# GpSimd's tensor work moved to VectorE, and a matmul cost in the list scheduler, in a two-block transformer kernel

## The chip, the cores and the metric

The kernel runs on one core of a Trainium2 chip. The metric is the device time of one execution in microseconds (us); lower is better. Measurements of this kernel repeat within about 0.1%.

## The reference

Two transformer blocks follow each other on 512 tokens of width 1024, in float32. Cut to what matters:

```
def first_block(x, c, ctx, ...):
    mod, mod_c = silu(c) @ w_ada + b_ada, silu(c_ctx) @ w_ada + b_ada     # shifts, scales, gates
    hc = modulate(rmsnorm(ctx, norm1_g), csh1, csc1)                       # context keys and values
    h = modulate(rmsnorm(x, norm1_g), sh1, sc1)
    q, k, v, hv, hx1, hx2, gna, ghy = split(h @ w_in)
    y_na = neighbourhood_attention(q, k, v, k_c, v_c, na_rpb)
    y_hy = hyena_mixer(hv, hx1, hx2, ...)          # short conv, sin-MLP filters, two long convs (DFT)
    x = x + g1 * gated_merge(gna, ghy, y_na, y_hy, w_na_o, w_hy_o, w_out)
    x = x + g2 * swiglu(modulate(rmsnorm(x, norm2_g), sh2, sc2), ffn_w1, ffn_w3, ffn_w2)
    return rmsnorm(x, final_g)

def second_block(x, mem, positions, ...):
    c_q, c_kv, k_r, u_ssm, x_q, gate_logits = split_combined(rmsnorm(x) @ w_in)
    y_a = mla_branch(...) @ w_o_mla                # latent attention, causal
    y_b = s5_branch(...) @ w_o_ssm                 # a complex linear recurrence over the tokens
    y_c = cross_branch(x_q, mem, ...) @ w_o_cross
    x = x + (gates0 * y_a + gates1 * y_b + gates2 * y_c) @ w_out
    g_ff, v_ff = split(causal_dwconv(rmsnorm(x) @ w_up))
    return x + (silu(g_ff) * v_ff) @ w_down
```

## The kernel before

**Rounded products.** A float32 matrix product is made of three products of rounded operands (type fp32r). ScalarE copies a tile into a rounded one (the high part), another engine subtracts it from the original (the low part, itself rounded), and TensorE accumulates high x high, high x low and low x high in a PSUM bank (`split`, `lo`, `mm`). Weights come in tiles of 128 x 1024 (`stream`): a load, a ScalarE cast and a subtraction for each tile, and then eight 128 x 128 stationary blocks, each used for 3 products of 128 x 512. Activations pass through the same split after each stage, in tiles of 128 x 512 (`pair`).

**No order is written by hand.** The program first records every instruction as a `Call` on an engine (`Trace.add`), with the pieces of memory that it reads and writes. `Trace.schedule` then plays a list schedule over the calls with a price for each (`Trace.time`) and a lag between engines; `Trace.plan` does this four times, forwards and backwards, and keeps the order with the shortest planned end; `emit` issues the calls in that order. Every instruction therefore has the source line of `emit`, L687, in the profile, and each engine runs its own queue strictly in the emitted order. SBUF is 96 pages of 128 x 512 in 48 segments (the tile `pages`), PSUM eight banks (`banks`), small columns lie in `small`; a call that needs a new page waits in the plan until one is free.

**Which engine.** Most calls name their engine. `may_swap` makes a `tensor_tensor` of VectorE or GpSimd with over 64 elements a row and no operand in PSUM a call of either engine; the plan sends it to GpSimd where it expects it to end there no later than on VectorE. Such calls are the `lo` subtractions, sums of squares, products in `cmul`, gates. Smaller `nc.gpsimd.tensor_tensor` and `tensor_copy` calls are GpSimd's outright. The plan lets a VectorE and a GpSimd instruction run side by side at full price each. A rounded product of n columns costs `n / 2.4 + 2.5` ns on TensorE in the plan, or `cols / 1.2` where that is more.

**Places that the prediction speaks of.** (1) `filters`, at the start: a two-layer sine MLP; each layer ends on VectorE with `sin_arg` (a range reduction of seven instructions of 128 x 256) and a sine on ScalarE; these calls are "urgent", so VectorE takes no others until they are done. Then come the splits of filter weights and DFT matrices, the modulation vectors, the first norm and the context norm (to 147 us). (2) `neighbourhood`, `branch_hy`, `merge1` and the norm of the memory tokens (338 to 530 us). (3) `s5`: products of the state input with phases, two scans over the chunks, and eight products or sums of 128 x 16 x 63 or 64 x 16 x 63 elements before TensorE can go on. (4) `mla`: per token block a small reciprocal square root in eight-element steps (`rsqrt`) and the eviction of heads from PSUM (`heads_to_rows`, 96 x 2 x 128).

```
def lo(self, out, src, hi, pool=None):
    e = self.nc.either if pool is None else self.nc.gpsimd if pool else self.nc.vector
    e.tensor_tensor(out=out, in0=src, in1=hi.bitcast(F32), op=ALU.subtract)
...
V.tensor_tensor(out=fr(F[0]), in0=fr(Z[0]), in1=fr(es if z else ec), op=ALU.mult)
G.tensor_tensor(out=fr(F[1]), in0=fr(Z[1]), in1=fr(ec if z else es), op=ALU.mult)
```

The functions that the diff touches, and what calls them:

Of the kernel before, what the change touches and what calls it, by code (L numbers as in the profile page):

```python
# [161 lines left out]
def layout(inp):  # L162
# [80 lines left out]
ENGINES = ("tensor", "vector", "scalar", "gpsimd", "sync")  # L243
# [7 lines left out]
    (1500.0, 2000.0, 1000.0, 1300.0, 2250.0),  # L251
)
ALONE = (DVE,)
DMA_START = 1700.0
RELEASE = 200.0, 150.0, 150.0, 100.0, 1200.0
TABLES = {AF.Silu: (0,), AF.Sin: (1, 0), AF.Exp: (2,), AF.Gelu_apprx_tanh: (3,)}
TABLE_LOAD = 1283.0
TICK, TICK_COLUMNS = 10240 / 3, 3060.0

# [70 lines left out]
class Call:  # L330
    __slots__ = ("engines", "engine", "name", "args", "kw", "time", "rank", "deps", "then", "waits", "pieces", "begun", "urgent", "start", "number", "tables", "columns")

# [127 lines left out]
class Trace:  # L460
# [15 lines left out]
    def time(engine, name, out, args, kw):  # L476

        n = out.free_size()
        if engine == PE:
            cols = args[1].ap.free_size()  # L480
            if name == "transpose":
                return max(2 * n / 2.4, 53)
            if args[1].ap.dtype == F32R:
                return max(n / 2.4 + 2.5, cols / 1.2)
            return max(4 * n / 2.4 + 2.5, cols / 0.6 if n < 16 else cols / 0.3 if cols > 64 else 54)
# [8 lines left out]
    @staticmethod  # L494
    def may_swap(engines, name, kw):

        views = [kw[n] for n in ("out", "in0", "in1") if n in kw]
        return engines in ((DVE,), (POOL,)) and name == "tensor_tensor" and kw["out"].ap.free_size() > 64 and not any(v.piece.bank for v in views)

    def add(self, engines, name, args, kw):  # L500
        if self.may_swap(engines, name, kw):
            engines = (DVE, POOL)
        c = Call()
# [7 lines left out]
        if name == "tensor_reduce" or name.startswith("reduce") or "accum_out" in kw:  # L511
            big = max((bare(x) for x in (*reads, *writes)), key=lambda x: x.free_size())
        c.time = [self.time(e, name, big, args, kw) for e in engines]
        deps, pieces = set(), {}
        for views, write in ((reads, False), (writes, True)):
# [19 lines left out]
    def schedule(self, order, back=False):  # L535
# [13 lines left out]
        fresh = [True] * len(ENGINES)  # L549
        until = [0.0] * len(ENGINES)  # L550
        events = []
        table = None
# [18 lines left out]
        while left or events:  # L571
            for e in range(len(ENGINES)):
                if not idle[e] or not (fresh[e] or e == POOL):
                    continue
                fresh[e], aside = False, []
                while ready[e]:
# [32 lines left out]
                    if not back:  # L609
# [3 lines left out]
                        if e == PE:  # L613
# [6 lines left out]
                            ticks[i + 1] += (1 - part) * c.columns  # L620
                    idle[e], until[e], fresh[e] = False, now + dur, True
                    n += 1
                    push(events, (now + dur, n, 0, c.number))
                    break
                for key in aside:
                    push(ready[e], key)
            if not events:
                if again:
                    return None
                again, fresh = True, [True] * len(ENGINES)  # L630
                continue
            again = False
            now = events[0][0]
            while events and events[0][0] <= now:
                _, _, kind, i = pop(events)
                c = calls[i]
                if kind == 2:
# [1658 lines left out]
```

## Time and profile before

| | |
|---|---|
| median of 3 runs | 1800.73 us (1799.32 to 1801.01) |
| the profiled execution | 1804.63 us, of which the span from first to last instruction is 1802.8 us |
| TensorE (PE) busy | 1720.8 us, 95% of the span, 8494 products |
| VectorE (DVE) busy | 1219.3 us, 68%, 2245 instructions |
| ScalarE (ACT) busy | 724.4 us, 40% |
| GpSimd (POOL) busy | 363.2 us, 20%, 297 instructions |
| moved by DMA | 235.44 MB, 130 GB/s over the span |
| mean granted TensorE clock | 0.984 of full speed |

TensorE is busy nearly all the time, so what can be won is mostly its 82 us of idle time, the stretches at half clock, and the start. An idle gap of TensorE names what ended it; VectorE ends most of them.

### The profile page before, as it was taken

The numbers are of one execution on the slowest core, as the hardware profiler recorded it, in microseconds if no ns is written. First come the engines' busy times: TensorE is split into PE (matmuls) and PEld (weight loads), VectorE is DVE, ScalarE is ACT, GpSimd is POOL, SyncE is SP. The second block draws the span as 40 slices with busy tenths as digits, with TensorE's granted clock in tenths as the row PEclk, the third lists the DMA queues.
The fourth block names the chain that finished last, engine by engine and source line by source line (L and its number), as shares of the span: only waits on it lengthen the run. The fifth ranks groups of instructions, "written<-read, shape, count | busy, mean of one in ns | idle before, by whom it ended". The sixth has DMA issues, their size and how long they took to land.

```text
span 1802.8 us, 23185 instructions
## 1 busy us (share of the span) xinstructions
PE 1720.8 (95%) x8494; PEld 1423.4 (79%) x8494; DVE 1219.3 (68%) x2245; ACT 724.4 (40%) x1199; POOL 363.2 (20%) x297
## 2 busy tenths in 40 slices
PE   4899999999979999999999999899989999999999
PEld 2478888788868888888888887788867888888887
DVE  7987794888897559435268636649998535896520
ACT  5543333655644222233234431445564413453320
POOL 6631321312240006101011002203242000120000
PEclk9899999999989999999999999999999999999999
DMA  6743233544842623424326434422257222221430
GB/s 224 251 139 117 82 130 108 195 146 141 307 173 104 222 100 94 131 97 137 115 79 208 136 111 126 141 71 72 71 174 270 105 82 71 79 74 70 139 113 18
DMA packets 93664, 235.44 MB, mean 131 GB/s; under 512 B 18316, under 2 KB 26252, under 8 KB 93550
## 3 DMA queue, kind: packets, MB, share of 16 engines
q1 hardware_dynamic: 93550, 233.95, 37.9%
q8 instruction: 67, 1.10, 0.2%
q14 instruction: 47, 0.39, 0.1%
HBM read 206.91 MB, written 27.00 MB: 130 GB/s over the span
## 4 chain that ended last, share of the span: by engine, by line
PE 81%; DVE 10%; DMA 2%; issue 2%; ACT 1%; SPq 0%; POOL 0%; DVEq 0%; POOLq 0%; ACTq 0%
PE banks L687 81%; DVE pages L687 8%; DVE small L687 1%; DMA pages<-in_w_out_dram 1%; ACT pages L687 1%; SPq L687 0%; DMA pages<-in_w_xq_dram 0%; DMA pages<-in_w_mem_dram 0%; DVE banks L687 0%; DMA pages<-s5g 0%; DMA pages<-in_w_ada_dram 0%; POOL pages L687 0%; DMA ud<-pages 0%; DVE gs L687 0%; DVE mod L687 0%
## 5 line engine op out<-in xcount | busy, mean ns | idle before, releaser
L687 PE MATMUL banks<-pages,pages 128*128 128x512 f32 (+6 forms) x7835 | 1676.5, 373 | 58.5 <-DVE pages L687 46.0
L687 PEld LDWEIGHTS banks<-pages,pages 128*128 128x128 f32 (+3 forms) x7835 | 1350.1, 186 | 335.6 <-DVE pages L687 57.5
L687 DVE TENSOR_TENSOR pages<-pages,pages 128x1024 fp32r<-128x1024 f32 (+12 forms) x574 | 572.5, 1020 | 114.2 <-ACT pages L687 102.7
L687 ACT CAST pages<-pages 128x1024 fp32r<-128x1024 f32 (+5 forms) x471 | 398.3, 871 | 399.2 <-DVE pages L687 93.8
L687 POOL TENSOR_TENSOR pages<-pages,pages 128x512 fp32r<-128x512 f32 (+11 forms) x187 | 306.9, 1650 | 939.8 <-ACT pages L687 538.2
L687 DVE TENSOR_TENSOR pages<-banks,pages 128x512 fp32r<-128x512 f32 (+8 forms) x219 | 111.4, 522 | 117.0 <-PE banks L687 91.5
L687 DVE TENSOR_TENSOR pages<-banks,R 128x512 f32<-128x512 f32 x81 | 57.0, 707 | 131.1 <-PE banks L687 130.8
L687 ACT ACTIVATE pages<-pages 128x512 f32<-128x512 f32 (+4 forms) x91 | 50.4, 570 | 168.2 <-DVE pages L687 158.5
L687 ACT ACTIVATE pages<-banks 128x512 f32<-128x512 f32 (+4 forms) x75 | 37.3, 511 | 181.4 <-PE banks L687 154.4
L687 ACT COPY pages<-banks 128x512 f32<-128x512 f32 (+6 forms) x121 | 57.8, 502 | 103.1 <-PE banks L687 100.8
L687 DVE SCALAR_TENSOR_TENSOR pages<-pages,vec,pages 128x511 f32<-128x511 f32 (+3 forms) x120 | 94.0, 801 | 6.9 <-ACT pages L687 5.8
L687 ACT ACTIVATE pages<-pages,vec 128x512 f32<-128x512 f32 (+1 forms) x84 | 63.4, 766 | 68.0 <-DVE pages L687 66.8
L687 DVE TENSOR_TENSOR pages<-pages,banks 128x512 f32<-128x512 f32 x66 | 43.9, 681 | 60.1 <-PE banks L687 58.5
L687 PE MATMUL banks<-ident,pages 128*128 128x128 f32 (+2 forms) x464 | 72.5, 276 | 7.2 <-DVE pages L687 5.7
L687 POOL MEMSET pages<- 128x1 f32 (+4 forms) x63 | 28.9, 482 | 236.8 <-PE banks L687 135.3
L687 PEld LDWEIGHTS banks<-ident,pages 128*128 128x128 f32 (+2 forms) x464 | 56.5, 145 | 22.5 <-issue 5.6
L687 ACT CAST pages<-banks 128x512 fp32r<-128x512 f32 (+5 forms) x118 | 53.2, 469 | 37.5 <-PE banks L687 26.6
L687 ACT ACTIVATE pages<-banks,small 128x512 f32<-128x512 f32 (+3 forms) x80 | 46.4, 585 | 24.9 <-DVE small L687 24.5
L687 DVE SCALAR_TENSOR_TENSOR pages<-pages,pages 128x1024 bf16<-128x1024 f32 (+2 forms) x39 | 52.8, 1367 | 0.1
L687 DVE SCALAR_TENSOR_TENSOR pages<-banks,mod,pages 128x512 f32<-128x512 f32 x16 | 12.0, 750 | 43.7 <-PE banks L687 43.7
L687 DVE SCALAR_TENSOR_TENSOR pages<-pages,banks 128x512 f32<-128x512 f32 x40 | 26.9, 678 | 9.3 <-PE banks L687 9.3
L687 DVE SCALAR_TENSOR_TENSOR small<-small 128x4 f32<-128x4 f32 (+2 forms) x150 | 30.4, 211 | 1.8
(79 smaller groups left out, 464.0 us busy)
## 6 DMA issues: line engine op xcount, KB each, us to landing
pages<-in_w_f_dram SPq DMA_DIRECT2D x66, 512.0 KB, 4.0
pages<-in_w_ada_dram SPq DMA_DIRECT2D x48, 512.0 KB, 5.9
pages<-in_w_up_dram SPq DMA_DIRECT2D x44, 512.0 KB, 3.2
pages<-in_w_g_dram SPq DMA_DIRECT2D x24, 512.0 KB, 4.3
pages<-in_w_down_dram SPq DMA_DIRECT2D x22, 512.0 KB, 3.4
pages<-in_w_out_dram SPq DMA_DIRECT2D x16, 512.0 KB, 6.9
pages<-in_w_hy_dram SPq DMA_DIRECT2D x12, 512.0 KB, 4.3
pages<-in_w_na_dram SPq DMA_DIRECT2D x12, 512.0 KB, 4.0
```

The costliest lines, as they stand in the source:

```text
L687: self.tc.keep_in_program_order(f(*map(at, c.args), **{k: at(v) for k, v in c.kw.items()}))
```

## The change

GpSimd keeps 63 memsets and the identity matrix. Its 228 `tensor_tensor` and `tensor_copy` calls, fixed or swapped, become VectorE's: `may_swap` is gone, and `add` rewrites the engine. The scheduler learns a shared port between VectorE and GpSimd (`shares_port`), but a GpSimd call takes part in it only if it reads a tensor, and none of the remaining ones does, so these lines decide nothing here. A rounded product now costs `n / 2.4 + 13.3` ns in the plan, that is 226.6 ns for 512 columns where it was 215.8. VectorE's prices are as before. The calls themselves, 12,416 of them, are the same.

```diff
+APART = 0.7
...
+WEIGHTS = 13.3
...
             if args[1].ap.dtype == F32R:
-                return max(n / 2.4 + 2.5, cols / 1.2)
+                return max(n / 2.4 + WEIGHTS, cols / 1.2 + 5.0)
...
     @staticmethod
-    def may_swap(engines, name, kw):
-
-        views = [kw[n] for n in ("out", "in0", "in1") if n in kw]
-        return engines in ((DVE,), (POOL,)) and name == "tensor_tensor" and kw["out"].ap.free_size() > 64 and not any(v.piece.bank for v in views)
+    def shares_port(engine, name, reads, writes):
+
+        tensors = [v for v in reads if v.shape[-1] > 1 or len(v.shape) > 2]
+        if engine == POOL:
+            return bool(tensors)
+        return engine == DVE and bool(tensors) and not any(v.piece.bank for v in (*tensors, *writes))
 
     def add(self, engines, name, args, kw):
-        if self.may_swap(engines, name, kw):
-            engines = (DVE, POOL)
+        if engines[-1] == POOL and name in ("tensor_tensor", "tensor_copy"):
+            engines = (DVE,)
...
                     ok = c.urgent or not (e in ALONE and urgent[e] or any(all(calls[d].begun for d in u.deps) for u in urgent[e]))
-                    if e == POOL and not urgent[DVE] and not back and len(c.engines) > 1:
-                        wait = sum(calls[i].time[0] for r, i in ready[DVE] if r < c.rank and not calls[i].begun)
-                        ok = max(until[DVE], now) + wait + c.time[0] >= now + dur
+                    if ok and not back and e in (DVE, POOL) and c.ports[c.engines.index(e)]:
+                        other = port[DVE + POOL - e]
+                        if other > now:
...
+                                dur += other - now
```

The order of all engines is planned anew. At three places this is what stands there.

**VectorE's queue behind the urgent sine MLP, before.** The first two rows are the end of `sin_arg` and the low parts of the hidden layer; then low parts of the filter weights (1024 wide) and the first products with PSUM:

```order
L687 TENSOR_SCALAR pages_167<-pages_167 128x256
L687 TENSOR_TENSOR pages_188<-pages_167,pages_188 64x256 x2
L687 MEMSET ones 128x2
L687 TENSOR_TENSOR pages_204<-pages_146,pages_163 128x1024
L687 TENSOR_TENSOR pages_213<-pages_161,pages_177 128x1024
L687 TENSOR_SCALAR pages_151<-pages_151 1x1024
L687 TENSOR_TENSOR pages_238<-banks_65,pages_154 128x512
```

The same place now:

```order
L714 TENSOR_SCALAR pages_165<-pages_165 128x256
L714 TENSOR_TENSOR pages_179<-pages_165,pages_179 64x256 x2
L714 MEMSET ones 128x2
L714 TENSOR_TENSOR pages_179<-pages_134,pages_144 128x512
L714 TENSOR_TENSOR pages_193<-pages_134,pages_144 128x512
L714 TENSOR_TENSOR pages_193<-pages_138,pages_153 128x512
L714 TENSOR_TENSOR pages_203<-pages_138,pages_153 128x512
L714 TENSOR_TENSOR pages_208<-pages_122,pages_147 128x1024
L714 TENSOR_TENSOR pages_214<-pages_122,pages_147 128x1024
L714 TENSOR_SCALAR pages_155<-pages_155 1x1024
L714 TENSOR_TENSOR pages_227<-pages_208,pages_216 128x1024
L714 TENSOR_TENSOR pages_236<-pages_214,pages_221 128x1024
```

Four low parts of 512 columns (DFT matrices) and two sums of 1024 (filter weights) that GpSimd worked on during the sine MLP now stand behind it, ahead of the casts and low parts that TensorE's first products need.

**VectorE's queue in `s5`, before.** The first rows end the phase products, then two scans (printed as SCALAR_TENSOR_TENSOR of 128x1024), then the products and sums with 63 columns:

```order
L687 TENSOR_TENSOR pages_8510<-pages_8362,pages_7949 128x1024
L687 TENSOR_TENSOR pages_7872<-banks_65,pages_8053 128x512
L687 TENSOR_TENSOR pages_7164<-banks_65,pages_8011 128x512
L687 TENSOR_TENSOR pages_8478<-pages_7930,pages_7872 128x512
L687 TENSOR_TENSOR pages_8326<-pages_7164,pages_7930 128x512
L687 SCALAR_TENSOR_TENSOR pages_7769<-pages_8216,pages_8478 128x1024
L687 SCALAR_TENSOR_TENSOR pages_8545<-pages_8216,pages_8326 128x1024
L687 TENSOR_TENSOR pages_7930<-pages_7769,pages_8011 128x16x63
L687 TENSOR_TENSOR pages_8563<-pages_8545,pages_8011 128x16x63
L687 TENSOR_TENSOR pages_8466<-pages_8545,pages_8053 128x16x63
L687 TENSOR_TENSOR pages_7901<-pages_8362,pages_8563 64x16x63
L687 TENSOR_TENSOR pages_7901<-pages_7930,pages_8466 64x16x63
```

The same place now:

```order
L714 TENSOR_TENSOR pages_8429<-pages_8049,pages_4828 128x512
L714 TENSOR_TENSOR pages_8437<-pages_6830,pages_8260 128x512
L714 SCALAR_TENSOR_TENSOR pages_8068<-pages_8167,pages_8429 128x1024
L714 SCALAR_TENSOR_TENSOR pages_7409<-pages_8167,pages_8437 128x1024
L714 TENSOR_TENSOR pages_8494<-pages_8068,pages_8012 128x16x63
L714 TENSOR_TENSOR pages_8429<-pages_7409,pages_8034 128x16x63
L714 TENSOR_TENSOR pages_8167<-pages_8068,pages_8034 128x16x63
L714 TENSOR_TENSOR pages_8437<-pages_7409,pages_8012 128x16x63
L714 TENSOR_TENSOR pages_8137<-pages_8494,pages_8429 64x16x63
L714 TENSOR_TENSOR pages_8137<-pages_8167,pages_8437 64x16x63
```

One of the four 128 x 16 x 63 products came from GpSimd's queue before and stands between its neighbours now; the unrelated 128 x 1024 low part has left the stretch.

**VectorE's queue in `mla`, before**, between the last steps of an `rsqrt` (`small`, 128x8) and an eviction of heads (96x2x128, here the last row) that TensorE waits for:

```order
L687 SCALAR_TENSOR_TENSOR small_64<-small_64 128x8
L687 SCALAR_TENSOR_TENSOR pages_9989<-banks_65,vec,pages_9403 96x2x128
L687 SCALAR_TENSOR_TENSOR small_64<-small_64 128x8
L687 TENSOR_REDUCE small_64<-banks_65 128x1
L687 TENSOR_TENSOR small_64<-small_64 128x8
L687 TENSOR_TENSOR pages_8739<-pages_9914,pages_9714 128x1024
L687 SCALAR_TENSOR_TENSOR small_64<-small_64 128x8
L687 SCALAR_TENSOR_TENSOR pages_9607<-banks_65,vec,pages_9593 96x2x128
L687 SCALAR_TENSOR_TENSOR small_64<-small_64 128x8
L687 SCALAR_TENSOR_TENSOR pages_9791<-banks_65,vec,pages_9671 96x2x128
```

The same eviction now is the last row here:

```order
L714 TENSOR_REDUCE small_64<-banks_65 128x1
L714 SCALAR_TENSOR_TENSOR small_64<-small_64 128x8
L714 TENSOR_TENSOR pages_9229<-pages_9229,pages_9914 128x512
L714 TENSOR_SCALAR small_64<-small_64 128x1
L714 TENSOR_TENSOR small_64<-small_64 128x8
L714 SCALAR_TENSOR_TENSOR small_64<-small_64 128x8 x2
L714 SCALAR_TENSOR_TENSOR pages_8995<-banks_65,vec,pages_8971 96x2x128
```

One sum of 512 columns that was GpSimd's stands ahead of it now; the 128 x 1024 low part, the two other evictions and three of the small steps have gone elsewhere.

**Counts.** Between the same two instructions of the program, VectorE's queue holds: from the last row of the hidden layer's low parts (ended at 23.3 us) to the end of the context norm's `rsqrt` (147.1 us) 24 instructions of 1024 columns, 93 of about 512, none of about 256 and 39 small ones before, and 33, 114, 7 and 34 now; from 337.8 us (a low part of attention weights) to 530.4 us (the last step of the memory norm's `rsqrt`) 44, 93, 66 and 66 before, and 55, 109, 75 and 65 now; from 1248.6 to 1352.4 us (in `mla`) 5, 39, 111 and 130 before, and 9, 45, 114 and 125 now.

## Rows read from the trace of the kernel before

**Rows 1.** The page, busy us (share of the span) and instructions by engine.

```profile
PE 1720.8 (95%) x8494; PEld 1423.4 (79%) x8494; DVE 1219.3 (68%) x2245; ACT 724.4 (40%) x1199; POOL 363.2 (20%) x297
```

**Rows 2.** Windows: stretch, length, busy (instructions) of PE, PEld, DVE, ACT, POOL; clock.

```profile
23.30:147.10 123.80, 106.98 (x466) 74.64 (x464) 117.79 (x158) 66.41 (x101) 68.94 (x38) 0.93 0.50 169
337.80:530.40 192.60, 178.31 (x919) 149.43 (x919) 170.84 (x323) 101.56 (x189) 58.41 (x36) 0.97 0.56 198
530.40:950.00 419.60, 419.51 (x2001) 348.64 (x2002) 243.40 (x520) 134.56 (x187) 63.77 (x76) 0.99 0.35 120
1107.80:1132.20 24.40, 16.84 (x152) 12.80 (x147) 24.31 (x22) 2.58 (x4) 13.19 (x5) 0.94 0.36 109
1248.60:1352.40 103.80, 93.92 (x530) 80.54 (x530) 97.33 (x315) 67.20 (x170) 33.94 (x25) 0.97 0.33 113
```

**Rows 3.** The chain that ended last, its last long piece: start, us, what.

```profile
1383.66 415.45 PE banks L687 x1824
```

**Rows 4.** Groups by form: count, busy us, mean ns; the last from 840 to 890 us.

```profile
L687 POOL TENSOR_TENSOR pages<-pages,pages 128x1024 fp32r<-128x1024 f32 x34 | 90.7, 2671 | 91.2 <-ACT pages L687 56.3 <-PE banks L687 29.0 <-DVE pages L687 5.8
L687 DVE TENSOR_TENSOR pages<-pages,pages 128x1024 fp32r<-128x1024 f32 x255 | 332.0, 1311 | 76.5 <-ACT pages L687 72.4 <-PE banks L687 3.6
...
L687 DVE TENSOR_TENSOR pages<-pages,pages 128x1024 fp32r<-128x1024 f32 x13 | 15.8, 1223 | 18.4 <-ACT pages L687 14.7 <-PE banks L687 3.6
```

**Rows 5.** Timeline of the sine MLP: VectorE in each layer, GpSimd, TensorE's next product.

```profile
5.11 0.62 DVE L687 TENSOR_SCALAR pages<-pages 128x256 f32<-128x256 f32 x2
5.77 1.34 DVE L687 SCALAR_TENSOR_TENSOR pages<-pages 128x256 f32<-128x256 f32 x3
...
14.37 2.36 DVE L687 TENSOR_SCALAR pages<-pages 128x256 f32<-128x256 f32 x2
16.77 4.17 DVE L687 SCALAR_TENSOR_TENSOR pages<-pages 128x256 f32<-128x256 f32 x3
...
10.65 10.00 POOL L687 TENSOR_TENSOR pages<-pages,pages 128x1024 f32<-128x1024 f32 x6 [8.32 <-DMA pages<-in_hy_w_dram]
...
22.66 3.35 PE L687 MATMUL banks<-pages,pages 128*128 128x512 f32 x7 [8.90 <-DVE pages L687]
```

**Rows 6.** Timeline of s5: VectorE, GpSimd, TensorE.

```profile
1108.40 2.46 DVE L687 TENSOR_TENSOR pages<-banks,pages 128x512 f32<-128x512 f32 x4
...
1117.74 4.46 DVE L687 TENSOR_TENSOR_SCAN pages<-pages,pages 128x1024 f32<-128x1024 f32 x2
1122.12 13.28 DVE L687 TENSOR_TENSOR pages<-pages,pages 128x1008 f32<-128x1008 f32 x6
...
1120.10 4.25 POOL L687 TENSOR_TENSOR pages<-pages,pages 128x1008 f32<-128x1008 f32 x1 [3.43 <-DVE pages L687]
...
1132.18 4.10 PE L687 MATMUL banks<-pages,pages 128*64 128x128 f32 x17 [7.56 <-DVE pages L687]
```

**Rows 7.** Timeline of mla: ScalarE, VectorE, GpSimd, TensorE.

```profile
1306.17 1.55 ACT L687 ACTIVATE pages<-banks,vec 96x256 fp32r<-96x256 f32 x4 [0.23 <-PE banks L687]
...
1306.51 2.23 DVE L687 SCALAR_TENSOR_TENSOR small<-small 128x8 f32<-128x8 f32 x1
...
1312.20 2.35 DVE L687 TENSOR_TENSOR pages<-pages,pages 128x1024 fp32r<-128x1024 f32 x1
...
1315.02 0.47 DVE L687 SCALAR_TENSOR_TENSOR pages<-banks,vec,pages 96x256 fp32r<-96x256 f32 x1
...
1305.07 8.41 POOL L687 TENSOR_TENSOR pages<-pages,pages 128x512 f32<-128x512 f32 x5 [2.23 <-DMA pages<-br]
...
1315.55 2.72 PE L687 MATMUL banks<-pages,pages 128*128 128x384 f32 x6 [6.15 <-DVE pages L687]
```

**Rows 8.** Windows at half clock, columns as in Rows 2.

```profile
57.40:71.10 13.70, 12.70 (x40) 5.84 (x41) 13.26 (x13) 9.60 (x14) 8.49 (x5) 0.50 0.72 248
1129.20:1136.00 6.80, 3.71 (x17) 3.34 (x18) 6.74 (x3) 0.00 (x0) 5.05 (x2) 0.50 0.23 79
1313.50:1320.30 6.80, 4.75 (x15) 4.01 (x16) 5.61 (x21) 1.50 (x5) 0.00 (x0) 0.50 0.16 48
```

More of the change, by code (lines that the diff above doesn't have):

```diff
@@ L330 @@
 class Call:
-    __slots__ = ("engines", "engine", "name", "args", "kw", "time", "rank", "deps", "then", "waits", "pieces", "begun", "urgent", "start", "number", "tables", "columns")
+    __slots__ = ("engines", "engine", "name", "args", "kw", "time", "rank", "deps", "then", "waits", "pieces", "begun", "urgent", "start", "number", "tables", "columns", "ports")
 class Arena:
@@ L513, in add @@
         c.time = [self.time(e, name, big, args, kw) for e in engines]
+        views = lambda xs: [x for x in xs if isinstance(x, View)]
+        c.ports = [self.shares_port(e, name, views(reads), views(writes)) for e in engines]
         deps, pieces = set(), {}
@@ L550, in schedule @@
         until = [0.0] * len(ENGINES)
+        port = [0.0] * len(ENGINES)
         events = []
@@ L574, in schedule @@
                     continue
-                fresh[e], aside = False, []
+                fresh[e], aside, retry = False, [], 1e18
                 while ready[e]:
@@ L582, in schedule @@
                     ok = c.urgent or not (e in ALONE and urgent[e] or any(all(calls[d].begun for d in u.deps) for u in urgent[e]))
-                    if e == POOL and not urgent[DVE] and not back and len(c.engines) > 1:
-                        wait = sum(calls[i].time[0] for r, i in ready[DVE] if r < c.rank and not calls[i].begun)
-                        ok = max(until[DVE], now) + wait + c.time[0] >= now + dur
+                    if ok and not back and e in (DVE, POOL) and c.ports[c.engines.index(e)]:
+                        other = port[DVE + POOL - e]
+                        if other > now:
+                            if e == DVE and any(not calls[i].ports[0] and not calls[i].begun for r, i in ready[DVE]):
+                                ok = False
+                                retry = min(retry, other)
+                            else:
+                                dur += other - now
+                    if ok and e == POOL and not back and len(c.engines) > 1:
+                        mine = [calls[i] for r, i in ready[DVE] if not calls[i].begun]
+                        apart = sum(d.time[0] for d in mine if not d.ports[0])
+                        apart += max(0.0, until[DVE] - now) if port[DVE] <= now else 0.0
+                        wait = sum(d.time[0] for d in mine if d.rank < c.rank)
+                        ok = not urgent[DVE] and apart >= dur * APART and max(until[DVE], now) + wait + c.time[0] >= now + dur
                     new = [p for p in c.pieces if p.at is None]
@@ L621, in schedule @@
                     idle[e], until[e], fresh[e] = False, now + dur, True
+                    if not back and e in (DVE, POOL) and c.ports[c.engines.index(e)]:
+                        port[e] = now + dur
                     n += 1
@@ L626, in schedule @@
                     push(ready[e], key)
+                if idle[e] and retry < 1e18:
+                    n += 1
+                    push(events, (retry, n, 4, e))
             if not events:
@@ L635, in schedule @@
                 _, _, kind, i = pop(events)
+                if kind == 4:
+                    fresh[i] = True
+                    continue
                 c = calls[i]
```

## The prediction

> **What bounds the kernel now.** I read the page first: TensorE is busy 1720.8 of 1802.8 us [rows 1], so 82 us are idle, and nothing but those, the half-clock windows and TensorE's own pace can be won. The pace is fixed: in its last long piece the chain is 1824 products in 415.45 us [rows 3], 227.8 ns each, and from 530.4 to 950 us TensorE is busy 419.51 of 419.60 us [rows 2]. Where the gaps lie is the second reading, the windows: 16.8 us of them from 23.3 to 147.1 us, 14.3 from 337.8 to 530.4, 7.6 around `s5`, 9.9 from 1248.6 to 1352.4 [rows 2], and 22.7 before TensorE's first long run [rows 5]. In each of these stretches VectorE is nearly full: 117.79 of 123.80 us, 170.84 of 192.60, 24.31 of 24.40, 97.33 of 103.80 [rows 2]. So it is VectorE's queue that TensorE waits for, and GpSimd, 20% busy [rows 1], is not the bound itself.
>
> The third reading, the timelines, tells why VectorE is full. In the first layer of the sine MLP GpSimd does nothing, and VectorE's two scalings and three corrections take 0.62 and 1.34 us; in the second GpSimd is at work from 10.65 to 20.65 us, and the same instructions take 2.36 and 4.17 us [rows 5]. A step of eight elements takes 2.23 us while GpSimd runs from 1305.07 to 1313.48 us, and a low part of 1024 columns 2.35 [rows 7], where one from a stretch with a single GpSimd product takes 1.223 [rows 4]. So a VectorE instruction with its operands in SBUF waits while a GpSimd one runs: GpSimd's help is paid for in VectorE's time. I call that the lock.
>
> **The change, part by part.** VectorE gets 228 instructions and loses the lock. What is one worth? Back to back, four of 512 columns take 2.46 us [rows 6], 0.60 each; two of 256 columns 0.62 [rows 5], 0.31 each. On that line one of 1024 is 1.19, just under the 1.223 that it takes alone [rows 4]; on GpSimd it takes 2.671 [rows 4]. A small one I put at 0.10. I call the sum by these prices the clean work; busy time over it is lock, with some dependent steps that cannot overlap. The counts are those between the same two instructions in the two orders.
>
> *Start, to 147.1 us.* Without the lock the second sine layer is 2.36 + 4.17 - 0.62 - 1.34 = 4.6 us shorter [rows 5]. Nothing else stands in VectorE's queue there, so all of it counts. From 23.3 us on, 24 x 1.19 + 93 x 0.60 + 39 x 0.10 = 88.3 us of clean work were 117.8 us busy [rows 2]: 29.5 us of lock. The queue now holds 33 x 1.19 + 114 x 0.60 + 7 x 0.31 + 34 x 0.10 = 113.2 us, 24.9 more. Net -4.6, together -9. TensorE's first long run starts no earlier: it waits now for four low parts (2.4 us), a sum (1.2) and a cast (about 1, the cost of a sum less some) that were done ahead, which eats the 4.6 us at that one place; but VectorE is saturated behind it, and TensorE needs only 107 of the 124 us, so the end of the stretch follows VectorE's sum. Bounds: 0, if the lock was no one's delay, and -16.8, all of TensorE's idle time [rows 2].
>
> *337.8 to 530.4 us.* Clean 44 x 1.19 + 93 x 0.60 + 66 x 0.31 + 66 x 0.10 = 135.2, busy 170.8 [rows 2]: 35.6 us above clean. Added: 11 x 1.19 + 16 x 0.60 + 9 x 0.31 - 0.1 = 25.4. At face value -10. But VectorE is idle for 21.8 us here, waiting for others, and isolated instructions cost more than clean, so part of the 35.6 is no lock. I take -3; bounds +25.4 (no lock comes off the path) and -14.3 (all of TensorE's idle time).
>
> *`s5`.* From 1107.8 to 1132.2 us VectorE never rests, and TensorE stands for the last 7.56 us [rows 2, 6]. The queue up to the instruction that TensorE waits for now holds 13 of 512 columns, two scans (4.46 together, one without GpSimd beside it) and five of 1008: 7.8 + 4.5 + 5 x 1.19 = 18.2 us instead of 24.4. That includes the product that GpSimd made in 4.25 us [rows 6], the only one in a second queue that the chain needs. So -6 of 7.6, with 0 as the other bound.
>
> *`mla`.* ScalarE has made the high parts of four evictions by 1307.72 us, but VectorE makes the low part that TensorE waits for at 1315.02, behind locked eight-element steps and a locked 1024 low part of weights; TensorE idles 6.15 us [rows 7]. Now one 512 sum (0.60) and four small steps stand ahead of it, and the 1024 one does not. The stretch as a whole: clean 5 x 1.19 + 39 x 0.60 + 111 x 0.31 + 130 x 0.10 = 76.8, busy 97.3 [rows 2]; added 4 x 1.19 + 6 x 0.60 + 3 x 0.31 - 0.5 = 8.8. Many steps here depend on each other, so the 20.5 are not all lock. I take -5; bounds +8.8 and -9.9 (TensorE's idle time).
>
> [...]
>
> *The product's price in the plan* executes nothing. The plan's product of 512 columns is now 226.6 ns, by the row 227.8 [rows 3]; before it was 215.8, so in that last piece alone the plan saw TensorE 22 us ahead of the truth. It alters orders everywhere, and I put no term on it: TensorE's full stretches have no gap to close, and what it may do elsewhere is in the range. GpSimd's memsets stay and cost VectorE nothing that I can see. Loads and casts are the same instructions.
>
> **Sum.** -9 - 3 - 6 - 5 - 2 = -25 us. The profiled execution took 1804.6, so 1779.6; the median of the runs shown, 1800.7, is 3.9 lower, so **1776 us**.
>
> [...]
>
> **Rivals.**
>
> *The moved instructions cost more than their clean price.* VectorE waits 72.4 us for ScalarE's casts before its 255 low parts of 1024 columns [rows 4], 0.28 us each. GpSimd waited for casts in a queue of its own; now such a wait holds up all that stands behind it on VectorE. The three stretches take in 32, 35 and 8 more instructions: 75 x 0.28 = 21 us on VectorE, and 14 at the end if two thirds of it fall where TensorE waits: **1790**. Against: the plan knows casts and their lags, and puts a low part where its cast is over. [...]
>
> *Nothing changes.* What GpSimd gave and what its lock took are equal, VectorE's busy time stays at 1219 us [rows 1] and the gaps stay with it: **1800**. For it: 24.9 against 29.5 at the start. Against: in `s5` and `mla` the lock fell on instructions that TensorE waited for, and what came in instead is shorter or stands behind.
>
> *Slower: the moved work stands ahead of the evictions and the lock returns nothing there.* From 337.8 to 530.4 us VectorE's queue grows by 25.4 us, in `mla` by 8.8. If the lock hit only low parts of weights made long ahead, while evictions out of PSUM passed, those 34 us are added where VectorE is full: 1776 + 3 + 5 + 34 = **1818**. It decides from the point where the lock returns less than half of the added work in the two stretches. For it: GpSimd is busy 58.4 us in the first [rows 2], and its time there bought work at no visible price wherever VectorE read PSUM. Against: eight-element steps of `rsqrt`, on which whole norms wait, were among those locked [rows 7]. [...]
>
> *More.* With VectorE's durations as planned, the plan comes true in the middle stretch too (-10 instead of -3) and the clock stays up (-8 instead of -2), and the start reaches its bound: **1755**.
>
> **How the numbers follow.** The forecast, 1762 to 1789: 0.62. Costlier instructions 0.10, more 0.11, nothing changes 0.08, slower 0.09. Anything within 0.2% (3.6 us) cannot be told from no change. So faster 0.83, same 0.08, slower 0.09. The range goes from the largest gain, 1754, to 1797, where "nothing changes" begins; likeliest 1776.
>
> **What will show it.** Right: VectorE's 1024 low parts at a mean of 1.22 us where they had 1.311; the second sine layer as short as the first; the context norm's last step some 9 us earlier; TensorE's gap in `s5` at 1 to 2 us and the one at 1315 us gone; VectorE's busy time within 10 us of 1219; TensorE's idle time at 60 us or less. Wrong: VectorE over 90% busy from 338 to 530 us with more TensorE gaps there than 14 us; new gaps in the stretch from 530 to 950 us, which had none; a load that comes late because pages are held longer.

## The result, and the profile after

The changed kernel takes **1758.42 us** (median of 4 executions, 1750.54 to 1758.82) beside 1800.03 us for the kernel before (1798.34 to 1801.01): ratio 0.9759, 95% interval 0.9731 to 0.9788. The forecast was 1776 with the range 1754 to 1797.

| profiled execution | before | after |
|---|---|---|
| span | 1802.8 us | 1756.9 us |
| TensorE busy, the same 8494 products | 1720.8 | 1710.2 |
| TensorE idle (span less busy) | 82.0 | 46.7 |
| VectorE busy | 1219.3 | 1194.7 |
| GpSimd busy | 363.2 | 29.2 |
| mean granted clock | 0.984 | 0.993 |

Of the 45.9 us between the spans, 35.3 are idle time of TensorE and 10.6 are busy time: the same products ran with less half clock. The page of after, its engines:

```profile
PE 1710.2 (97%) x8494; PEld 1416.4 (81%) x8494; DVE 1194.7 (68%) x2473; ACT 729.7 (42%) x1204; POOL 29.2 (2%) x69
```

VectorE has 228 instructions more and is busy 24.6 us less, so what it shed was more than what it took on. The clearest group, of after (form, count, busy us, mean ns), answers to [rows 4]:

```profile
L714 DVE TENSOR_TENSOR pages<-pages,pages 128x1024 fp32r<-128x1024 f32 x289 | 349.2, 1217 | 64.4 <-ACT pages L714 45.5 <-issue 9.7 <-PE banks L714 8.4
```

34 more low parts of 1024 columns, and a mean of 1217 ns where it was 1311. The start of after, as [rows 5]: both layers of the sine MLP on VectorE, then TensorE's first long run.

```profile
4.98 0.62 DVE L714 TENSOR_SCALAR pages<-pages 128x256 f32<-128x256 f32 x2
5.64 1.34 DVE L714 SCALAR_TENSOR_TENSOR pages<-pages 128x256 f32<-128x256 f32 x3
...
15.94 0.62 DVE L714 TENSOR_SCALAR pages<-pages 128x256 f32<-128x256 f32 x2
16.59 1.34 DVE L714 SCALAR_TENSOR_TENSOR pages<-pages 128x256 f32<-128x256 f32 x3
...
25.27 6.10 PE L714 MATMUL banks<-pages,pages 128*128 128x512 f32 x16 [9.95 <-ACT pages L714]
```

The second layer takes what the first does, 0.62 and 1.34 us instead of 2.36 and 4.17, but it starts 1.57 us later, at 15.94 us instead of 14.37, and the long run starts at 25.3 us where it was 22.7: the casts and low parts that now stand behind the layer hold it. It is behind this that time comes back. The context norm's last step, of before and then of after:

```profile
146.99 0.15 DVE L687 SCALAR_TENSOR_TENSOR small<-small 128x2 f32<-128x2 f32 x1
```

```profile
137.51 0.15 DVE L714 SCALAR_TENSOR_TENSOR small<-small 128x2 f32<-128x2 f32 x1
```

Since the order is another, the stages are best cut where TensorE has done the same sum of products, each counted at its unstalled length (the counts of products differ by up to 3%, since the mix of short and long ones is another). First windows of before with these cuts, then those of after (columns as in [rows 2]). The window of after from 505.10 us, the full stretch, answers to the third of [rows 2].

```profile
23.30:196.90 173.60, 153.78 (x762) 116.97 (x760) 154.78 (x205) 89.72 (x142) 83.03 (x48) 0.95 0.47 157
196.90:337.10 140.20, 140.18 (x769) 121.77 (x769) 100.47 (x150) 57.46 (x96) 27.85 (x31) 0.99 0.35 121
337.10:538.90 201.80, 187.07 (x949) 156.25 (x948) 178.72 (x340) 107.73 (x202) 62.07 (x39) 0.96 0.54 193
957.20:1094.60 137.40, 136.76 (x706) 115.96 (x705) 82.43 (x214) 52.15 (x100) 10.84 (x10) 0.99 0.45 144
1107.80:1136.00 28.20, 20.52 (x168) 16.12 (x164) 28.08 (x23) 2.58 (x4) 15.32 (x5) 0.88 0.31 94
1248.80:1356.20 107.40, 96.34 (x544) 82.39 (x544) 100.67 (x319) 67.58 (x171) 33.94 (x25) 0.97 0.33 114
```

```profile
20.30:185.50 165.20, 150.08 (x769) 116.78 (x770) 156.77 (x255) 88.98 (x136) 0.53 (x6) 0.97 0.52 177
185.50:325.80 140.30, 140.16 (x788) 121.34 (x787) 111.01 (x206) 68.39 (x123) 4.99 (x16) 1.00 0.30 98
325.80:505.10 179.30, 179.16 (x925) 151.09 (x924) 150.24 (x304) 98.35 (x174) 2.00 (x5) 1.00 0.64 233
505.10:924.00 418.90, 418.90 (x1995) 347.43 (x1994) 226.60 (x481) 135.43 (x189) 0.96 (x1) 1.00 0.35 118
924.00:1067.00 143.00, 140.97 (x718) 118.74 (x716) 97.56 (x326) 50.75 (x98) 2.88 (x3) 0.96 0.48 150
1079.00:1104.20 25.20, 21.47 (x172) 17.35 (x168) 25.07 (x29) 4.64 (x6) 0.96 (x1) 0.93 0.43 125
1214.70:1312.70 98.00, 95.64 (x541) 80.41 (x540) 95.04 (x333) 64.96 (x165) 7.64 (x8) 1.00 0.33 113
```

| stage | before | after | difference | forecast, the clock's -2 apart |
|---|---|---|---|---|
| start, up to the cut | 196.9 | 185.5 | -11.4 | -9 |
| middle | 201.8 | 179.3 | **-22.5** | **-3** |
| second block's first norm | 137.4 | 143.0 | **+5.6** | 0 |
| `s5` | 28.2 | 25.2 | -3.0 | -6 |
| `mla` | 107.4 | 98.0 | -9.4 | -5 |

The stretches that the table leaves out gave the other 5.2 us, none of them more than 2.4. About half of the gain lies in the middle stretch: TensorE was idle 14.7 of its 201.8 us and is idle 0.14 now, and its busy time fell by 7.9 us besides, at clock 1.00 instead of 0.96. The new order also took work out of it: VectorE and GpSimd together run 309 instructions there where they ran 379, and 222 instead of 181 in the stretch before, in which TensorE is full either way. Two half-clock windows of before that lay in this stretch:

```profile
501.10:507.90 6.80, 5.38 (x13) 4.30 (x14) 6.80 (x10) 1.76 (x3) 3.15 (x3) 0.50 0.70 242
528.40:535.20 6.80, 4.71 (x12) 3.79 (x13) 6.80 (x15) 5.38 (x10) 2.21 (x2) 0.50 0.53 216
```

And the stretch that lost, of after: TensorE's timeline (start, us, what, idle time before it), then its two half-clock windows.

```profile
924.17 1.95 PE L714 MATMUL banks<-ones,pages 128*128 128x2 f32 x16
926.05 8.00 PE L714 MATMUL banks<-pages,pages 128*32 128x16 f32 x30
...
951.07 1.47 PE L714 MATMUL banks<-ones,pages 128*128 128x2 f32 x8 [1.68 <-ACT pages L714]
```

```profile
927.60:931.00 3.40, 3.40 (x10) 2.63 (x9) 3.23 (x10) 0.09 (x1) 0.00 (x0) 0.50 0.55 187
951.50:958.30 6.80, 6.80 (x20) 5.54 (x20) 2.88 (x12) 1.28 (x3) 0.00 (x0) 0.50 0.19 75
```

Half of those 10.2 busy us, 5.1, is what the half clock cost here, an estimate from two groups: 14 products of 128x512 took 6.2 us in the second window, 0.44 each, where 1719 took 394.2 us from 505.10 to 924.00 us, 0.23 each. Beside the kernel before, whose clock in this stage was 0.99, TensorE is busy 4.2 us more and idle 1.4 us more, together the 5.6 that the stage lost. The first half-clock window lies among products of 512 columns (10 of them; the row of 926.05 us prints the form of its first product), right behind those of 2 and 16, with no idle time of TensorE in it; the second began after a wait of 1.68 us.

`s5` and `mla` of after, as [rows 6, 7]: VectorE's first instruction of the `s5` stretch, the scans and VectorE's products with 63 columns, TensorE behind them, and TensorE around the head product that had waited 6.15 us.

```profile
1079.57 0.67 DVE L714 TENSOR_TENSOR pages<-pages,R 32x512 f32<-32x512 f32 x1
...
1086.77 4.46 DVE L714 TENSOR_TENSOR_SCAN pages<-pages,pages 128x1024 f32<-128x1024 f32 x2
...
1091.15 9.35 DVE L714 TENSOR_TENSOR pages<-pages,pages 128x1008 f32<-128x1008 f32 x8
...
1098.08 12.10 PE L714 MATMUL banks<-pages,pages 128*64 128x128 f32 x58 [3.73 <-DVE pages L714]
...
1274.60 2.62 PE L714 MATMUL banks<-pages,pages 128*128 128x512 f32 x11
...
1277.19 3.64 PE L714 MATMUL banks<-pages,pages 128*128 128x512 f32 x14
```

The wait in `s5` is 3.73 us where it was 7.56; the one in `mla` is gone.

### The profile page after: what moved, and what is told of

Read it like the earlier page. It is cut to its first block, busy times and chain, and to the rows that moved or that the text cites. A ratio compares the mean times of both kernels' runs of the same rounds, so it can differ in the third digit from the quotient of the medians.

```text
span 1756.9 us, 22940 instructions
## 1 busy us (share of the span) xinstructions
PE 1710.2 (97%) x8494; PEld 1416.4 (81%) x8494; DVE 1194.7 (68%) x2473; ACT 729.7 (42%) x1204; POOL 29.2 (2%) x69
## 5 line engine op out<-in xcount | busy, mean ns | idle before, releaser
L714 PE MATMUL banks<-pages,pages 128*128 128x512 f32 (+5 forms) x7830 | 1663.5, 372 | 30.9 <-ACT pages L714 21.3
L714 PEld LDWEIGHTS banks<-pages,pages 128*128 128x128 f32 (+3 forms) x7830 | 1343.0, 185 | 305.8 <-ACT pages L714 25.3
L714 DVE TENSOR_TENSOR pages<-pages,pages 128x1024 fp32r<-128x1024 f32 (+12 forms) x747 | 616.7, 855 | 99.0 <-ACT pages L714 69.7
L714 ACT CAST pages<-pages 128x1024 fp32r<-128x1024 f32 (+4 forms) x471 | 396.9, 871 | 350.9 <-PE banks L714 111.6
L714 DVE TENSOR_TENSOR pages<-banks,pages 128x512 fp32r<-128x512 f32 (+7 forms) x219 | 111.8, 523 | 95.4 <-PE banks L714 73.4
L714 ACT ACTIVATE pages<-banks 128x512 f32<-128x512 f32 (+4 forms) x75 | 37.6, 512 | 227.8 <-PE banks L714 220.3
L714 DVE SCALAR_TENSOR_TENSOR pages<-pages,vec,pages 128x511 f32<-128x511 f32 (+3 forms) x114 | 82.6, 745 | 3.3 <-ACT pages L714 2.6
L714 DVE SCALAR_TENSOR_TENSOR pages<-pages,pages 128x1024 bf16<-128x1024 f32 (+3 forms) x42 | 42.9, 1021 | 1.6 <-DMA gna<-pages 1.4
L714 DVE TENSOR_TENSOR pages<-pages 128x16 f32<-128x16 f32 (+6 forms) x107 | 29.3, 308 | 1.8 <-DMA pages<-in_eye_dram 1.5
L714 DVE TENSOR_REDUCE small<-banks 128x1 f32<-128x256 f32 (+3 forms) x64 | 27.9, 447 | 0.3
```

The lines of the kernel that those rows point to most:

```text
L714: self.tc.keep_in_program_order(f(*map(at, c.args), **{k: at(v) for k, v in c.kw.items()}))
```

## The experiments

The change has three parts: the lock goes (GpSimd no longer reads SBUF beside VectorE), the order is planned anew, and the plan's product is dearer. Theory A is that the lock's removal makes the gain. Its rivals give it to the price or to the new order. Medians below stand against 1801.1, 1802.4 and 1801.4 us for the kernel before in the three series.

**Price alone** (`e1_price`, on the kernel before; the line `WEIGHTS = 13.3` is left out here):

```diff
-                return max(n / 2.4 + 2.5, cols / 1.2)
+                return max(n / 2.4 + WEIGHTS, cols / 1.2 + 5.0)
```

> The kernel before with only the plan's price of a rounded product changed (226.6 ns for 512 columns); GpSimd keeps its tensor work, so the order is planned anew with both engines. Theory A, the lock (VectorE's instructions stand still while GpSimd's run, and that is what TensorE waited for): within 10 us of before, 1790 to 1808, VectorE's 1024 low parts still at 1.3 us in the mean. Theory B, the truer price is what closes TensorE's gaps: 1775 or less.

Measured 1825.51 us (1824.95 to 1826.67), ratio 1.0138 [1.0122, 1.0154]. The dearer product by itself makes the kernel slower by 24 us, which lies outside of what either theory gave. VectorE's low parts of 1024 columns stayed at a mean of 1308 ns, as theory A had it.

**Move alone** (`e2_move`, on the changed kernel): the old price back, all else as changed.

```diff
-                return max(n / 2.4 + WEIGHTS, cols / 1.2 + 5.0)
+                return max(n / 2.4 + 2.5, cols / 1.2)
```

> The changed kernel with the plan's old price of a rounded product (215.8 ns): only the move of GpSimd's tensor work. Theory A (the lock): 1755 to 1772, nearly all of the gain. Theory B (the price): 1785 or more. If the two parts need each other: between, 1772 to 1785.

Measured **1747.12 us** (1746.91 to 1747.78), ratio 0.9702 [0.9687, 0.9717]. The interval lies below that of the change as made: this version beats both kernels, and the price took 11 us of what the move gave. The time also lies below theory A's range, by 8 us.

**The lock alone, old order** (`e3_old_order`, on the kernel before): planned as before, GpSimd's tensor instructions issued on VectorE at the place that the plan gave them.

```diff
-            f = getattr(getattr(self.nc, ENGINES[c.engine]), c.name)
+            e = DVE if c.engine == POOL and c.name in ("tensor_tensor", "tensor_copy") else c.engine
+            f = getattr(getattr(self.nc, ENGINES[e]), c.name)
```

> The kernel before in its own order, planned for both engines, but each tensor instruction of GpSimd is issued on VectorE at the place where the plan has it start. Nothing is planned anew. Theory A (the lock): the lock is gone whatever the order, so at least half of the gain is there, 1780 or less. Theory C (the new plan is what gains, since it knows that VectorE has all the work): 1795 or more, because VectorE's queue is longer and in an order meant for two engines.

Measured 1771.21 us (1768.67 to 1780.68), ratio 0.9845 [0.9814, 0.9876]: -30 us with nothing replanned. Because the order is that of before, its windows hold nearly the same products as those of [rows 2] (the third, `s5`, ends behind TensorE's wait, as the one of before from 1107.80 us):

```profile
20.10:137.10 117.00, 104.13 (x465) 74.58 (x464) 114.04 (x195) 66.23 (x101) 0.00 (x0) 0.97 0.55 190
324.90:511.00 186.10, 177.86 (x919) 148.54 (x919) 168.35 (x354) 102.19 (x190) 2.09 (x4) 0.98 0.58 206
1083.40:1109.00 25.60, 19.72 (x169) 15.68 (x164) 25.48 (x27) 2.56 (x4) 0.96 (x1) 0.87 0.34 101
1220.40:1320.50 100.10, 92.39 (x525) 77.89 (x526) 95.61 (x334) 66.54 (x169) 7.55 (x8) 1.00 0.34 114
```

The first, second and fourth stand against 123.80, 192.60 and 103.80 us: -6.8, -6.5 and -3.7, and the first window begins 3.2 us earlier. TensorE's idle time fell by 4.0, 6.1, 1.8 and 2.2 us in the four. In the middle stretch VectorE does 31 instructions more and is busy 2.5 us less.

This run takes away two things at once, the lock and results that came later from GpSimd than they now come from VectorE. In the kernel before, the waits that a GpSimd result ended came to 0.3 us on TensorE, 5.6 on VectorE and 22.6 on ScalarE, so lateness can have had a part; this run does not set it apart.

**The lock back, new order** (`e4_new_order`, on the changed kernel): the 228 instructions that the kernel before had given to GpSimd are issued there again (`GPSIMD` lists their numbers; the list is left out), at their places in the new order.

```diff
-            f = getattr(getattr(self.nc, ENGINES[c.engine]), c.name)
+            e = POOL if c.number in GPSIMD else c.engine
+            f = getattr(getattr(self.nc, ENGINES[e]), c.name)
```

> The changed kernel in its own order, but the 228 instructions that GpSimd had before are issued on GpSimd again at the place where the plan has them start on VectorE. Theory A (the lock): slower than the change by 20 us or more, 1780 to 1810, with VectorE's 1024 low parts over 1.28 us in the mean. Theory C (the new plan): within 10 us of the change, 1768 or less.

Measured 1794.43 us (1791.68 to 1798.88), ratio 0.9968 [0.9955, 0.998]. The same order is 36 us slower with GpSimd at work than without, and the low parts of 1024 columns take 1303 ns again. Lateness counts here too: TensorE's waits for results of GpSimd came to 10.7 us. So in either order GpSimd's tensor work, with its lock and its late results together, costs 30 to 36 us more than its help is worth.

**Is it the reading of SBUF, or a busy GpSimd?** Two kernels add work for nobody to the changed kernel, at the same 109 places (the list `SHADOW` and the tile `shadow` are left out here). In `e5_shadow` GpSimd subtracts the two inputs of an instruction that VectorE has just been given, into a tile that nothing reads; in `e6_memsets` it copies one column and fills the tile three times.

```diff
+            if c.number in SHADOW:
+                x, y = at(c.kw["in0"]), at(c.kw["in1"])
+                self.tc.keep_in_program_order(self.nc.gpsimd.tensor_tensor(out=self.shadow[:, : x.free_size()], in0=x, in1=y, op=ALU.subtract))
```

```diff
+            if c.number in SHADOW:
+                x, y = at(c.kw["in0"]), at(c.kw["in1"])
+                self.tc.keep_in_program_order(self.nc.gpsimd.tensor_copy(self.shadow[:, :1], y[:, :1]))
+                for _ in range(3):
+                    self.tc.keep_in_program_order(self.nc.gpsimd.memset(self.shadow[:, : x.free_size()], 0.0))
```

> The changed kernel in its own order, all its work on VectorE, and beside it GpSimd repeats 109 of the tensor instructions that it had before (512 and 1024 columns, both inputs in SBUF) into a tile of its own that nobody reads. Theory A (the lock is what GpSimd's instructions cost): VectorE's 1024 low parts go up to 1.28 us or more, and the time to 1775 or more, though VectorE has the same instructions in the same order. Theory D (GpSimd slowed the kernel by being late with results that others needed): 1764 or less, since nobody needs the copies.

> As the run with the repeated instructions, but at each of the 109 places GpSimd copies one column of the same input (so that it comes at the same time) and then writes its own tile three times with a constant: about as long busy, hardly reading. Theory A, in the form that only an instruction that reads SBUF tensors locks: 1765 or less, 1024 low parts at 1.24 us or less. If any busy GpSimd slows VectorE: as slow as the run with the repeated instructions, 1775 or more.

Measured 1837.01 us (1830.92 to 1839.15), ratio 1.0192 [1.0166, 1.0217], for the subtractions, and 1767.77 (1764.64 to 1770.25), ratio 0.9817 [0.9795, 0.984], for the fills: +79 and +9 us on the changed kernel. GpSimd was busy 253.8 us in the first and 318.0 in the second; VectorE, with the same instructions in the same order, was busy 1301.3 and 1196.1 us, where it is 1194.7 in the changed kernel. The sine MLP's second layer, first with the subtractions, then with the fills:

```profile
12.96 7.44 POOL L727 TENSOR_TENSOR shadow<-pages,pages 128x512 f32<-128x512 f32 x4 [0.43 <-ACT pages L724]
...
15.04 3.10 DVE L724 TENSOR_SCALAR pages<-pages 128x256 f32<-128x256 f32 x2
18.17 3.43 DVE L724 SCALAR_TENSOR_TENSOR pages<-pages 128x256 f32<-128x256 f32 x3
```

```profile
15.34 1.71 POOL L729 MEMSET shadow<- 128x512 f32 x3
...
16.01 1.19 DVE L724 TENSOR_SCALAR pages<-pages 128x256 f32<-128x256 f32 x2
...
17.24 1.34 DVE L724 SCALAR_TENSOR_TENSOR pages<-pages 128x256 f32<-128x256 f32 x3
17.36 1.69 POOL L729 MEMSET shadow<- 128x512 f32 x3
```

Beside subtractions the two scalings and three corrections take 3.10 and 3.43 us, beside fills 1.19 and 1.34 (0.62 and 1.34 alone). So theory A holds for the corrections, which have two inputs in SBUF: the subtractions, which read SBUF, held them up by 2.09 us, and the fills beside them by nothing. The eight-element steps of `rsqrt`, also with two inputs, say the same; the group in the kernel before, after the change, with the subtractions and with the fills:

```profile
L687 DVE SCALAR_TENSOR_TENSOR small<-small 128x8 f32<-128x8 f32 x48 | 11.8, 247 | 0.6
```

```profile
L714 DVE SCALAR_TENSOR_TENSOR small<-small 128x8 f32<-128x8 f32 x48 | 7.4, 159 | 0.3
```

```profile
L724 DVE SCALAR_TENSOR_TENSOR small<-small 128x8 f32<-128x8 f32 x48 | 10.7, 228 | 0.3
```

```profile
L724 DVE SCALAR_TENSOR_TENSOR small<-small 128x8 f32<-128x8 f32 x48 | 7.4, 161 | 0.3
```

The scalings, with one input, are another kind: beside fills they took 1.19 us instead of 0.62. The changed kernel has a case of it without any added work, a scaling of 512 columns beside three of the memsets that GpSimd kept:

```profile
1183.33 2.73 POOL L714 MEMSET pages<- 32x1024 f32 x3 [0.45 <-PE banks L714]
...
1184.26 2.08 DVE L714 TENSOR_SCALAR pages<-pages 128x512 f32<-128x512 f32 x1 [0.20 <-ACT pages L714]
```

The same scaling takes 0.43 us elsewhere in this kernel; here it ends at 1186.34 us, 0.28 behind the last memset. So fills, too, held up an instruction of one input, though all of that is little: VectorE's busy time rose by 1.4 us in all with the 327 fills and 109 copies.

Could the subtractions have slowed the kernel by keeping pages in use? In `e5_shadow` the waits that one of them ended came to 3.1 us on VectorE and 1.8 on ScalarE, against 106.6 us by which VectorE's own instructions became longer in sum. The fills cost 9 us, a little more than expected. There VectorE waited 11.0 us and ScalarE 8.8 for the one-column copies, which stand behind the fills in GpSimd's queue; that these waits are the 9 us is my reading.

**GpSimd's help with a plan that knows the lock** (`e7_aware_swap`): the old price, and `tensor_tensor` calls without PSUM may again go to either engine, with the new port rule and `APART` = 0.7 in the plan.

```diff
+        if PE not in engines and self.may_swap(engines, name, kw):
+            engines = (DVE, POOL)
+        elif engines[-1] == POOL and name in ("tensor_tensor", "tensor_copy"):
-        if engines[-1] == POOL and name in ("tensor_tensor", "tensor_copy"):
```

> GpSimd may take tensor instructions over 64 columns again (99 in this plan), but the plan knows the lock: it gives GpSimd one only where VectorE has enough work of instructions with PSUM operands beside it. Price of a rounded product as in the kernel before. To be held against the run that only moves (1747 us). Theory A, the lock cannot be planned around, because the plan's times drift from the true ones: 1755 or more. Theory E, a plan that knows the lock makes GpSimd's help worth something: 1745 or less.

Measured 1755.24 us (1753.29 to 1755.82), ratio 0.9741 [0.9723, 0.976]. The plan sent 99 instructions to GpSimd, and the kernel is 8 us slower than `e2_move`. So help from GpSimd, planned with the lock in view, gained nothing here. That it costs 8 us is not shown: the plan is another one too, and two plans without such help differ by as much (prices 0 and 2.5 below).

**The price again, with the move in place.** Three prices, to see whether dearer is slower. Each is one line on the changed kernel:

```diff
-WEIGHTS = 13.3
+WEIGHTS = 24.0
```

> The changed kernel with the plan's price of a rounded product at 237.3 ns for 512 columns (24.0 in place of 13.3). The price 215.8 gave 1747 us, 226.6 gives 1758. Theory F, a dearer product in the plan makes a worse order: 1765 or more. Theory G, any other price is only another order, as good or bad by chance: anywhere from 1740 to 1775, not in step with the price.

> The changed kernel with the plan's price for a weight change at 0 instead of 13.3 ns, all else as changed. So far, with the move of the tensor work in place, 2.5 ns gave 1747, 13.3 gave 1758 and 24 gave 1771 us. Theory F (the dearer the plan thinks TensorE is, the later it puts what TensorE waits for, so the time rises with the price): at or below 1749 us. Theory C (each price only draws another order, and the three points fell in step by chance): more than 4 us off the straight line through them, that is above 1749 or below 1740 us; F has no reason for a value above 1751.

> The changed kernel with the plan's price for a weight change at 7.9 instead of 13.3 ns, halfway between the old and the new price. Theory F: between 1749 and 1756 us. Theory C: outside of that, as likely above the 1758 of the dearer price as below the 1747 of the cheaper one.

| price, ns | 0 | 2.5 | 7.9 | 13.3 | 24 |
|---|---|---|---|---|---|
| median, us | 1755.39 | 1747.12 | 1756.1 | 1758.42 | 1771.11 |
| ratio to before | 0.974 | 0.9702 | 0.9743 | 0.9759 | 0.9831 |

Theory F (dearer is later) held at 24, which is clearly worse than the rest, and fell at 0: that gave 1755.39 us, above the 1749 that it allowed, and its 95% interval, 0.9724 to 0.9756, lies above that of 2.5. 7.9 came out at 1756.1, the upper edge of F's range, and decides nothing. So from 0 to 13.3 the price draws one order or another, 1747 to 1758 us, not in step with it. (At 2.5 the form was the old one, without the 5.0 in its second term.) Why the order at 2.5 is the best, and why 13.3 alone cost the kernel before 24 us, stays open.

## Why the prediction was right, point by point

The sign, the mechanism and the range held; the likeliest value was 18 us too high, and the time lies below the band from 1762 to 1789 that had most of the chances. That it lies in the range at all owes something to luck: with the old price the same move gave 1747, below the range's 1754, and the price, to which no term was given, brought it back. One table shows the parts (profiled executions, us):

| kernel | span | TensorE busy | idle |
|---|---|---|---|
| before | 1802.8 | 1720.8 | 82.0 |
| `e3_old_order` (lock gone) | 1769.2 | 1709.3 | 59.9 |
| after | 1756.9 | 1710.2 | 46.7 |
| `e2_move` | 1746.0 | 1702.4 | 43.6 |
| `e4_new_order` (lock back) | 1793.4 | 1715.3 | 78.1 |
| `e5_shadow` | 1834.3 | 1737.6 | 96.7 |

*The lock.* The four stall terms were -9 - 3 - 6 - 5 = -23 us of idle time, and in the old order the lock's removal took 22.1 us off TensorE's idle time. The reasoning from clean prices to lock was right in kind; that the sums agree so closely is partly luck. In the old order the start gave about 7 of its 9 us, the middle stretch 6.1 for 3, `s5` 1.8 for 6 and `mla` 2.2 for 5, and some 5 came from stretches that had no term. That GpSimd's memsets cost VectorE nothing was nearly so: a scaling waited 1.65 us for them at 1184 us.

*The clock.* The sum's last term, -2, and the -8 that "more" has in its place stand for the clock, and no run shows either. What the runs showed is that TensorE's busy time fell by 11.5 us with the lock gone, at a mean clock of 0.994, and by 10.6 in the change, at 0.993. Beside the three half-clock windows [rows 8] there were more, such as the two at 501 and 528 us shown above. The mean clock showed it beforehand: 0.016 x 1802.8 = 29 us were missing from full clock, which makes 58 us at 0.50, an estimate, and the three windows make up 27.3 of them. After the change it is 0.007 x 1756.9 = 12 that are missing.

*Start.* -9 forecast; the context norm's last step came 9.5 us earlier ("some 9"), and up to the cut at 185.5 us it was 11.4. The pieces: the second sine layer was 4.6 us shorter, as said, but began 1.57 us later, so that 3.0 of it are left at the end of the hidden layer's low parts; from there on 6.4 us came back where 4.6 were forecast (123.80 and 117.40 us, the latter shown below). The long run started no earlier, as said.

*337.8 to 530.4 us.* This is the step that failed in size: "I take -3", because VectorE's idle time there and isolated instructions cost more than clean. Measured -22.5: -14.6 of TensorE's idle time, all there was (the bound was -14.3), and -7.9 of its busy time, which no term of the stage counted. In the old order this stretch gave -6.5, halfway between the -3 and the face value of -10. The rest came with the new order, to which the prediction gave no term; with it VectorE and GpSimd run 70 instructions fewer here and 41 more in the stretch ahead. How much of the gain that is, no run shows. That an order planned without two engines side by side "at full price each" comes true more nearly is my reading, not shown apart from the order itself; with the lock put back in it the kernel lost 36 us again. VectorE is busy 84% of the stretch (150.24 of 179.30 us), below the 90% that was to prove me wrong.

*`s5`.* Forecast -6, measured -3.0, and a wait of 3.73 us where 1 to 2 were forecast. VectorE's queue became as short as was said: from its first instruction, now at 1079.57 us, to TensorE's product it is 18.5 us, 24.4 before, 18.2 forecast. But the new order gives TensorE 2.0 us less to do meanwhile (14.8 us where it had 16.8), so only 3.8 of the 5.9 us come off its wait.

*`mla`.* -5 forecast, -9.4 measured, close to its bound of -9.9; the wait at 1315 us is gone. In the old order it was -3.7, so the larger part came with the new one.

*The price.* "Executes nothing", and no term on it: that was wrong. It cost 11 us in the change and 24 us alone, through the order; why, no run shows. "TensorE's full stretches have no gap to close" held for 505 to 924 us, busy 418.90 of 418.90, but right behind it the new order lost 5.6 us.

*The count.* Of 1801 to 1758 us, taking the work off GpSimd gave -30 in the old order (the lock, with what lateness there was), the new order -24 at the old price, the new price +11. The forecast of -25 was nearest to that of the lock; "more", which had a chance of 0.11, at 1755, came nearest to the time, by its own words that the plan comes true in the middle stretch and the clock stays up.

*The rivals.* "Nothing changes" and "slower" fell: the lock returned more than the added work in the middle stretch. The one piece of "slower" that holds is that instructions that read PSUM pass: one group of them, with one input in PSUM (`banks`) and one in SBUF (`R`), 128x512, is 81 instructions of 707 ns before and after and of 706 in `e5_shadow`. That PSUM readers pass did not decide, because enough of what TensorE waits for has its inputs in SBUF. "The moved instructions cost more than their clean price" fell as well. Between the same two instructions, the hidden layer's low parts and the context norm's last step, the window of after is:

```profile
20.30:137.70 117.40, 102.28 (x472) 73.80 (x473) 112.27 (x190) 66.40 (x102) 0.00 (x0) 0.96 0.54 186
```

VectorE was busy 112.27 of 117.40 us, where the clean prices gave 113.2: in a queue that hardly rests, the back-to-back step, 2.46 us for four [rows 6], is the price that fits. The 0.10 us for a small instruction was assumed and stands in no row; the eight-element steps took 0.159 us after, which would add 2 us for the 34 small ones.

*Signs that missed.* VectorE's busy time was to stay within 10 us of 1219 and fell by 24.6; TensorE's wait in `s5`. The others came as said: 1217 ns a low part, TensorE idle for less than 60 us, no load that comes late (TensorE's waits that a load ended: 3.2 us, 3.4 before), no new gap in the stretch that lay from 530 to 950 us (505 to 924 now; the new gap at 951 us lies behind it).

## What to carry to other kernels

Before an elementwise instruction goes to GpSimd, read VectorE's same forms with and without GpSimd beside them: 228 helpers here kept GpSimd busy for 334 us, and the kernel was 30 to 36 us longer with them. To price such a change, first move it in the old order, and then let the planner loose: the first part can be reckoned, the second can only be measured. A planner's constant that is nearer to the measured duration (226.6 against 227.8 ns) is not thereby a better one; try a few values, since neighbouring ones gave times 2 to 13 us apart.

## What the runs showed of the hardware

A VectorE step of eight elements, 159 ns on average, rose to 228 beside GpSimd's subtractions in `e5_shadow` (247 in the kernel before) and stayed at 161 beside GpSimd's fills; a scaling of one input, 0.43 us, took 2.08 beside three memsets. TensorE's granted clock fell to 0.50 at 927.6 us of the changed kernel without an idle gap, during products of 512 columns right behind others of 2 and 16, and stood there for 37.5 us in one piece in `e5_shadow`:

```profile
57.10:94.60 37.50, 22.30 (x61) 6.77 (x60) 37.33 (x28) 14.18 (x19) 25.21 (x11) 0.50 0.53 176
```

In it VectorE was busy 37.33 us and TensorE 22.30: here the slower VectorE cost 15.2 us of TensorE's time idle, and about half of the 22.30, 11 us by the clock of 0.50, an estimate, again in products at half clock.
